# Dense expert dispatch on one core: gates loaded first, x in three loads, and a first store that waits for a load

## The chip, the cores and the metric

The kernel runs on one core of one Trainium2 chip. The metric is device time in microseconds (us) of one execution of the program; lower is better. A profiled execution also gives a span, from the first to the last instruction of the program, which is a little shorter than the device time of the same execution.

## The reference

```python
x: (8, 256, 512) float32;  gate_weights: (8, 256, 8) float32
gate_weights = gate_weights / (np.sum(gate_weights, axis=-1, keepdims=True) + 1e-8)
output = x[:, :, None, :] * gate_weights[:, :, :, None]     # (8, 256, 8, 512) float32
```

Every token has a row of 512 numbers and eight gates. The gates are normalised to a sum of one, and the row is written out eight times, once scaled by each gate. So 4.19 MB of x and 0.07 MB of gates come in, and 33.55 MB go out: the output is eight times as large as the input, and there is one multiplication for each number written.

## The kernel before, in words

**Tiling.** The 2048 tokens are dealt to 128 partitions, 16 consecutive ones to each. From here on "token j" means the j-th of the 16 of every partition, so one token is 128 rows of 512 numbers. All of x (`x_all`) and of the gates (`g_all`) fit into on-chip memory. The output doesn't; it goes through `ring`, which has ten slots of one token with its eight scaled copies (16 KB in each partition).

**Loads (L46 to L48).** ScalarE's queue (ACT) issues the gates. SyncE's queue (SP) issues the first five tokens of x (`HEAD = 5`) and then the other eleven. All of the 16 DMA engines serve both queues; in the profile SP's queue is q1 and ACT's is q10. Every DMA here is split by partition: eight of the 128 partitions fall to each DMA engine, and each partition's contiguous piece is one packet, which is called a row below. A DMA ends on each engine with a packet of 4 bytes, which counts up its semaphore; this is called the closing packet below.

**Gates (L53 to L56).** VectorE (DVE) sums the eight gates of each token, adds 1e-8, takes the reciprocal and multiplies: `gn`. Before that, L50 and L51 have ScalarE load its function table.

**Scaling.** A token is scaled in one of two ways: by eight single operations, one for each expert (`scale_one`: L63 on ScalarE, L65 on VectorE), or by one VectorE operation over all eight experts (`scale_token`, L68). Tokens 0 and 1 are split: experts 0 to 2 on ScalarE and 3 to 7 on VectorE. After that the first token of every chunk goes to ScalarE (L63, eight operations) and all others to VectorE (L68).

**Chunks and stores.** `CHUNKS` lists (first token, number of tokens, first slot). The five chunks hold 2, 3, 3, 4 and 4 tokens, in slots 0-1, 2-4, 5-7, 0-3 and 6-9. After each chunk SP issues one store of it (L87), when both engines are done with it. Chunk 3 writes over slots of chunks 0 and 1, so its operations wait until those stores have landed; chunk 4 writes over two slots of chunk 2 and waits for that store. Slots 8 and 9 are free from the start.

**What sets the order.** On an engine the instructions run in the order of the compiled program. The framework orders them by dependencies and its own estimate, and does not keep strictly to the source: the ten L68 operations run for tokens 3, 4, 6, 7, 14, 9, 15, 10, 11 and 13. SP's queue holds the two loads of x and the five stores in source order; an SP instruction that waits holds up all that come after it on SP.

Of the kernel before, what the change touches and what calls it, by code (L numbers as in the profile page):

```python
# [1 line left out]

# [4 lines left out]

SLOTS = 10
HEAD = 5
CHUNKS = ((0, 2, 0), (2, 3, 2), (5, 3, 5), (8, 4, 0), (12, 4, 6))  # L10


@with_exitstack
def kernel(
    ctx: ExitStack,
    tc: tile.TileContext,
    x: bass.AP,
    gate_weights: bass.AP,
    out: bass.AP,
):  # L20
    nc = tc.nc
    P = 128

    B, S, D = x.shape
    E = gate_weights.shape[-1]
    J = B * S // P

    fp32 = mybir.dt.float32
    mult = mybir.AluOpType.mult

    x_v = x.flatten_outer_dims().rearrange("(p j) d -> p j d", p=P)
    g_v = gate_weights.flatten_outer_dims().rearrange("(p j) e -> p j e", p=P)
    out_v = out.rearrange("b s e d -> (b s) e d").rearrange(
        "(p j) e d -> p j e d", p=P
    )

    pool = ctx.enter_context(tc.tile_pool(name="pool", bufs=1))

    g_all = pool.tile([P, J, E], fp32)
    x_all = pool.tile([P, J, D], fp32)  # L40
    ring = pool.tile([P, SLOTS, E, D], fp32)
    gsum = pool.tile([P, J, 1], fp32)
    gn = pool.tile([P, J, E], fp32)
    warm = pool.tile([P, 1], fp32)

    nc.scalar.dma_start(out=g_all, in_=g_v)  # L46
    nc.sync.dma_start(out=x_all[:, 0:HEAD, :], in_=x_v[:, 0:HEAD, :])
    nc.sync.dma_start(out=x_all[:, HEAD:J, :], in_=x_v[:, HEAD:J, :])  # L48

    nc.vector.memset(warm, 0.0)  # L50
    nc.scalar.copy(out=warm, in_=warm)  # L51

    nc.vector.reduce_sum(out=gsum, in_=g_all, axis=mybir.AxisListType.X)  # L53
    nc.vector.tensor_scalar_add(out=gsum, in0=gsum, scalar1=1e-8)  # L54
    nc.vector.reciprocal(out=gsum, in_=gsum)  # L55
    nc.vector.tensor_tensor(  # L56
        out=gn, in0=g_all, in1=gsum.to_broadcast([P, J, E]), op=mult
    )

    def scale_one(engine, j, e, slot):  # L60
        o_ap, s_ap = ring[:, slot, e, :], gn[:, j, e : e + 1]
        if engine is nc.scalar:
            nc.scalar.mul(out=o_ap, in_=x_all[:, j, :], mul=s_ap)  # L63
        else:
            nc.vector.tensor_scalar_mul(out=o_ap, in0=x_all[:, j, :], scalar1=s_ap)  # L65

    def scale_token(j, slot):
        nc.vector.tensor_tensor(  # L68
            out=ring[:, slot, :, :],
            in0=x_all[:, j : j + 1, :].to_broadcast([P, E, D]),  # L70
            in1=gn[:, j, :].unsqueeze(2).to_broadcast([P, E, D]),
            op=mult,
        )

    for j0, m, s0 in CHUNKS:
        for i in range(m):
            j, slot = j0 + i, s0 + i
            if j < 2:
                for e in range(E):
                    on_act = e < 3  # L80
                    scale_one(nc.scalar if on_act else nc.vector, j, e, slot)
            elif i == 0:
                for e in range(E):
                    scale_one(nc.scalar, j, e, slot)
            else:
                scale_token(j, slot)
        nc.sync.dma_start(  # L87
            out=out_v[:, j0 : j0 + m, :, :], in_=ring[:, s0 : s0 + m, :, :]
        )


# [1 line left out]
_INS = ['x', 'gate_weights']  # L93
_OUTS = [((8, 256, 8, 512), 'float32')]


# [23 lines left out]
```

## Time and profile before

| | us |
|---|---|
| median of 8 runs (lowest to highest) | 93.69 (93.59 to 93.81) |
| the profiled execution, device time | 93.61 |
| the profiled execution, span | 91.8 |
| device time outside the span | 1.8 |
| busy in the span: VectorE, ScalarE | 48.6, 25.1 |
| mean rate of all DMAs over the span | 412 GB/s |
| gates, from issue to landing | 5.9 |
| first load of x (1280 KB), from issue to landing | 5.7 |
| second load of x (2816 KB), from issue to landing | 12.0 |
| stores issued at | 11.90, 20.55, 29.22, 50.90, 57.25 |

Times inside the profile are counted from the first instruction. VectorE is busy for half of the span and ScalarE for a quarter, while DMA packets account for almost all of it. In the tables of windows (stretches of the span), "DMA share" is the time of all packets that start in a window, divided by 16 engines and the width of the window. It can be over 1 where many packets start together and run on beyond the window. Share times width is then the time that these packets take on one engine; the rate in GB/s times the width is the bytes that they carry.

### The profile page before, as it was taken

To read this page: it belongs to the slowest core of one execution; us is meant where nothing else is said; L and a number is where in the kernel's file an instruction comes from. 1 tells how busy PE (TensorE), PEld (TensorE's weight loads), DVE (VectorE), ACT (ScalarE), POOL (GpSimd) and SP (SyncE) were. 2 spreads that over 40 slices of the span, in tenths; PEclk is the share of its full clock that TensorE was granted. 3 is DMA by queue.
4 is the path that set the end of the run, shared out by engine and by line. 5 is a ranking of instruction groups with operands and counts; after the bars stand their busy time and mean duration, and the time that the engine had idled before them with its cause. 6 is when DMAs were issued, how large, how long until landed. Compare 5 with 4: busy or idle time off the path is not lost.

```text
span 91.8 us, 131 instructions
## 1 busy us (share of the span) xinstructions
DVE 48.6 (53%) x25; ACT 25.1 (27%) x40; POOL 0.2 (0%) x4
## 2 busy tenths in 40 slices
DVE  0019999999999999999999396000000000000000
ACT  5106999992992000000000299000000000000000
POOL 0000000000000000000000000000000000000000
DMA  4899889999779977987797999999993799999990
GB/s 71 342 490 422 373 385 457 457 457 571 343 343 535 492 343 343 664 364 343 343 685 343 457 457 457 457 457 457 457 428 143 343 457 457 457 457 457 457 457 0
DMA packets 1152, 37.81 MB, mean 412 GB/s; under 512 B 128, under 2 KB 256, under 8 KB 256
## 3 DMA queue, kind: packets, MB, share of 16 engines
q1 hardware_dynamic: 1008, 37.75, 96.1%
q10 hardware_dynamic: 144, 0.07, 0.2%
HBM read 4.26 MB, written 33.55 MB: 412 GB/s over the span
## 4 chain that ended last, share of the span: by engine, by line
DMA 31%; DVE 23%; ACT 5%; issue 2%; ACTq 1%; SPq 0%
DMA out_dram<-ring 25%; DVE ring L68 17%; DMA g_all<-in_gate_weights_dram 6%; ACT ring L63 5%; DVE ring L65 4%; ACTq L115 1%; DVE gn L56 0%; DVE gsum L53 0%; DVE gsum L55 0%; DVE gsum L54 0%; ACTq L63 0%; SPq L87 0%
## 5 line engine op out<-in xcount | busy, mean ns | idle before, releaser
L68 DVE TENSOR_TENSOR ring<-x_all,gn 128x4096 f32<-128x4096 f32 x10 | 43.5, 4421 | 1.4 <-DMA out_dram<-ring 1.4
L63 ACT ACTIVATE ring<-x_all,gn 128x512 f32<-128x512 f32 x38 | 23.6, 709 | 31.0 <-DMA out_dram<-ring 25.9
L65 DVE TENSOR_SCALAR ring<-x_all,gn 128x512 f32<-128x512 f32 x10 | 4.0, 482 | 0.0
L53 DVE TENSOR_REDUCE gsum<-g_all 128x16 f32<-128x128 f32 x1 | 0.3, 286 | 5.8 <-DMA g_all<-in_gate_weights_dram 5.8
L51 ACT ACT_TABLE_LOAD x1 | 1.3, 1283 | 1.1 <-PEq L104 1.1
L50 DVE MEMSET warm<- 128x1 f32 x1 | 0.1, 59 | 0.8 <-PEq L104 0.8
L56 DVE TENSOR_TENSOR gn<-g_all,gsum 128x128 f32<-128x128 f32 x1 | 0.3, 292 | 0.0
L55 DVE RECIPROCAL gsum<-gsum 128x16 f32<-128x16 f32 x1 | 0.3, 253 | 0.0
L51 ACT COPY warm<-warm 128x1 f32<-128x1 f32 x1 | 0.2, 191 | 0.0
L54 DVE TENSOR_SCALAR gsum<-gsum 128x16 f32<-128x16 f32 x1 | 0.2, 175 | 0.0
L104 POOL MEMSET const-bfloat16-1.0<- 128x1 bf16 x1 | 0.1, 102 | 0.0
L104 POOL MEMSET const-uint8-127<- 128x1 uint8 x1 | 0.1, 101 | 0.0
L104 POOL MEMSET const-float32-0.0<- 128x1 f32 x1 | 0.1, 99 | 0.2 <-issue 0.2
L104 POOL MEMSET const-float32-1.0<- 128x1 f32 x1 | 0.1, 98 | 0.0
## 6 DMA issues: line engine op xcount, KB each, us to landing
out_dram<-ring SPq DMA_DIRECT2D x2, 6144.0 KB, 20.0
out_dram<-ring SPq DMA_DIRECT2D x1, 4096.0 KB, 11.2
x_all<-in_x_dram SPq DMA_DIRECT2D x1, 2816.0 KB, 12.0
x_all<-in_x_dram SPq DMA_DIRECT2D x1, 1280.0 KB, 5.7
g_all<-in_gate_weights_dram ACTq DMA_DIRECT2D x1, 64.0 KB, 5.9
out_dram<-ring SPq DMA_DIRECT2D x2, 27.3
```

What stands on the lines that cost most here:

```text
L50: nc.vector.memset(warm, 0.0)
L51: nc.scalar.copy(out=warm, in_=warm)
L53: nc.vector.reduce_sum(out=gsum, in_=g_all, axis=mybir.AxisListType.X)
L54: nc.vector.tensor_scalar_add(out=gsum, in0=gsum, scalar1=1e-8)
L55: nc.vector.reciprocal(out=gsum, in_=gsum)
L56: nc.vector.tensor_tensor(out=gn, in0=g_all, in1=gsum.to_broadcast([P, J, E]), op=mult)
L63: nc.scalar.mul(out=o_ap, in_=x_all[:, j, :], mul=s_ap)
L65: nc.vector.tensor_scalar_mul(out=o_ap, in0=x_all[:, j, :], scalar1=s_ap)
L68: nc.vector.tensor_tensor(out=ring[:, slot, :, :], in0=x_all[:, j : j + 1, :].to_broadcast([P, E, D]), in1=gn[:, j, :].unsqueeze(2).to_bro ...
L104: nc = _bacc.Bacc("TRN2", target_bir_lowering=False, num_devices=1)
L115: with _tile.TileContext(nc) as tc:
```

## The change

The gates move from ACT's queue to SP's, ahead of everything there. The first load of x shrinks from five tokens to two (`HEAD = 2`, 1024 KB) and moves to ACT's queue. The rest of x is split at token 13 (`TAIL`): SP loads tokens 2 to 12 (2816 KB, called the body below) and then tokens 13 to 15 (768 KB, the tail). The store of chunk 0 gets a dependency on the body's load: SP may not issue it until the body has landed. Token 3 was one VectorE operation over all experts; now experts 0 and 1 of it go to ScalarE and 2 to 7 to VectorE, as single operations. Token 2 stays with ScalarE's eight operations. Operations, chunks, slots and stores are otherwise the same.

```diff
-HEAD = 5
+HEAD = 2
+TAIL = 13
...
-    nc.scalar.dma_start(out=g_all, in_=g_v)
-    nc.sync.dma_start(out=x_all[:, 0:HEAD, :], in_=x_v[:, 0:HEAD, :])
-    nc.sync.dma_start(out=x_all[:, HEAD:J, :], in_=x_v[:, HEAD:J, :])
+    nc.sync.dma_start(out=g_all, in_=g_v)
+    nc.scalar.dma_start(out=x_all[:, 0:HEAD, :], in_=x_v[:, 0:HEAD, :])
+    body_load = nc.sync.dma_start(
+        out=x_all[:, HEAD:TAIL, :], in_=x_v[:, HEAD:TAIL, :]
+    )
+    nc.sync.dma_start(out=x_all[:, TAIL:J, :], in_=x_v[:, TAIL:J, :])
...
+            elif j == 2:
+                for e in range(E):
+                    scale_one(nc.scalar, j, e, slot)
+            elif j == 3:
+                for e in range(E):
+                    scale_one(nc.scalar if e < 2 else nc.vector, j, e, slot)
             elif i == 0:
...
-        nc.sync.dma_start(
+        store = nc.sync.dma_start(
             out=out_v[:, j0 : j0 + m, :, :], in_=ring[:, s0 : s0 + m, :, :]
         )
+        if j0 == 0:
+            tc.add_manual_dep(
+                store.ins,
+                body_load.ins.name,
+                mybir.DependencyInfo(
+                    mybir.DependencyClass.Sync, mybir.DependencyReason.DATA
+                ),
+                reason="no store among the loads",
+            )
```

In the compiled order of the changed kernel VectorE runs 16 single operations instead of 10 and then L68 nine times, for tokens 4, 6, 7, 9, 14, 15, 10, 11 and 13. ScalarE runs 40 single operations instead of 38. SP's queue holds gates, body, tail and the five stores.

## The prediction, made before the changed kernel ran

> **What bounds the kernel now.** I begin with the page: the row of DMA slices, and the queues.
>
> ```profile
> DMA  4899889999779977987797999999993799999990
> ...
> q1 hardware_dynamic: 1008, 37.75, 96.1%
> ```
>
> Packets of SP's queue alone fill 96.1% of the 16 engines' span, while VectorE is busy for 53%. The low digits are coarse: a packet counts where it starts, and packets of 64 KB take 2.4 us. Next the chain of work, in order of time:
>
> ```profile
> 0.72 5.87 DMA g_all<-in_gate_weights_dram
> ...
> 7.76 4.05 DVE ring L65 x10
> 11.81 11.34 DVE ring L68 x3
> ...
> 29.22 22.91 DMA out_dram<-ring
> 52.13 0.02 issue
> ```
>
> It names gates, VectorE and a store, but is a chain of dependencies only. The store issued at 29.22 landed at 52.13 because it stood behind two others. What matters is when the DMA engines had nothing to move. The windows show it, first where the loads end and the first store begins, then where chunk 3's store begins:
>
> ```profile
> 12.38:12.48 0.10, 0.10 (x1) 0.10 (x1) 0.00 (x0) 1.00 0.05 0
> 12.48:12.58 0.10, 0.10 (x1) 0.10 (x1) 0.00 (x0) 1.00 0.02 0
> 12.58:12.68 0.10, 0.10 (x1) 0.10 (x2) 0.00 (x0) 1.00 0.02 0
> 12.68:12.74 0.06, 0.06 (x1) 0.06 (x2) 0.00 (x0) 1.00 0.01 0
> 12.74:12.90 0.16, 0.16 (x1) 0.16 (x2) 0.00 (x0) 1.00 7.60 3277
> ```
>
> ```profile
> 51.60:51.75 0.15, 0.00 (x0) 0.00 (x0) 0.00 (x0) 1.00 0.05 0
> 51.75:51.90 0.15, 0.00 (x0) 0.00 (x0) 0.00 (x0) 1.00 16.40 6991
> 54.20:54.36 0.16, 0.16 (x1) 0.16 (x1) 0.00 (x0) 1.00 15.15 6554
> ```
>
> The last two columns are DMA share and GB/s. From 12.38 to 12.74 no data packet starts; there are only closing packets of the loads, most of them early (mean 12.51). From 12.74 to 12.90 all 16 engines begin the store (3277 GB/s x 0.16 us = 16 rows of 32 KB), on the mean at 12.80. So **the engines idle 0.29 us on the mean**, and 0.16 us if the last closing is set against the last beginning. The second place is alike: closings about 51.66, beginnings about 51.81, 0.14 us. From 12.74 to 51.74 the share is 1.00, as from 51.75 to 90.48. The kernel is DMA traffic from end to end, and these two gaps and the start are all that an order of work can win.
>
> **Prices from the rows.** A 32 KB row takes 7.60 x 0.16 = 1.216 us on its engine, a 64 KB row 15.15 x 0.16 = 2.424. So data moves at 27.1 bytes per ns, with 0.008 us over for each row. By this a 10 KB row costs 0.386, one of 4 KB (new head) 0.16, of 6 KB (tail) 0.235, of 512 bytes (gates) 0.027; these are estimates. A row of the body has the 22 KB of the old second load. The first rows (window 1.74:2.20, share 2.14, so 0.98 us each) show 0.60 us of start-up. SP's issue to first row is 12.74 - 11.90 = 0.84 us. From the last closing packet to landing is 0.4 us (12.74, against 1.16 + 12.0).
>
> **Gates first, and a smaller head.** Before, gates rows alternate with 10 KB rows of x, so both land together: issue 0.72 + 5.9 for the gates, 0.73 + 5.7 for the head. After, if the two queues alternate again, eight pairs of 0.027 + 0.16 follow the start: 1.94 (mean first row) + 0.60 + 1.50 = 4.0, with spread and landing (0.7: before, gates and head close between 5.68 and 6.10, and the gates land at 6.6) **4.7 instead of 6.6**. The chain from gates to the first scaling is unchanged (7.76 - 6.59 = 1.17), so scaling starts at 5.9 and chunk 0 is ready to issue 4.14 us later, as now (11.90 - 7.76): 10.0. The gain is hidden by itself, because no store can move data before the loads are through. It is cover. Swapping queues costs no issue: SP still has its second DMA at 1.16, the tail's issue (0.43) follows at 1.6, and ACT's 0.39 comes ahead of the same table load.
>
> **Three loads.** Each engine serves 32 load rows instead of 24, and one closing packet more: 8 x 0.008 + 0.01 = **+0.07 us**, on the path. Otherwise the bytes are the same.
>
> Here a rule speaks against the change. The Trainium skill, "DMA: Bandwidth & Descriptors", section "Rules for kernel authors", asks for at least 1 MiB per DMA, and its section "Anatomy of one DMA" fits 2.0 us of fixed time to each DMA of the GpSimd path; the 768 KB tail would by that make the sum 95.4. But here the second load landed 6.7 us after the first (13.16 against 6.43) with 2.88 MB: 430 GB/s, hence no fixed time between queued DMAs.
>
> **The added wait.** Before, the loads' last closings lie from 12.38 to 12.74; after, 0.07 later. The body closes 8 x 0.235 + 0.01 = 1.89 earlier: 10.56 to 10.92. It lands at 11.3; SP issues about 0.07 later (52.13 to 52.21 is such a wake-up) at 11.4, and the first row is ready at 12.24, the last at 12.40. The loads end from 12.45 to 12.81, so **the first gap closes**, with 0.05 us to spare at the tightest. The tail covers the landing, the issue and the first row of the store. Behind the wait on SP stand only the four later stores, which nothing wants before 18. It binds (11.3 against 10.0), but 0.5 us before today's issue.
>
> **Tokens 2 and 3.** They now wait for the body: VectorE idles from 10.0 to 11.4 and ScalarE a little longer. Then VectorE does six single operations, 0.40 each by their spacing (4.05 for ten), then token 4 at 4.34 (39.10 for nine): 18.2. ScalarE does ten at 0.61: 17.5. Chunk 1 can be issued at 18.3 against 20.55, needed by 21.6 (chunk 0 ends near 22.5, less 0.84). Chunk 3 is complete after token 11, the eighth large operation: 11.4 + 2.4 + 8 x 4.34 = 48.5, against 50.90. Its store is needed by 51.66 - 0.84 = 50.8, less what the stream gains: 50.5. So **the second gap closes too**. Without this move chunk 3 would be at 11.4 + 9 x 4.34 = 50.5, on the edge. Waits on slots cost VectorE nothing: token 9 comes at 26.8 (chunk 0 landed by 23), token 10 at 39.8 (chunk 1 by 38).
>
> **The sum.** On the mean engine -0.29 - 0.14 + 0.07 = -0.36; on the slowest, -0.16 - 0.14 + 0.07 = -0.23. The last engine ends the kernel, but engines change places, so I take the middle, -0.30. The profiled execution (93.61, span 91.8 and 1.8 around it) becomes 93.31; it lay 0.08 under the median, so I forecast **93.4**. No row shows how the start-up changes with small rows: it may save some of its 0.60 or cost as much again. I take no change, since the first rows wait for a first read either way.
>
> **Rivals.**
> *The head comes late* (slower). Gates and body are in one queue. If the head's rows come a little later, the gates' rows are through first, and the head's rows alternate with 22 KB rows of the body, 0.835 us each. With n such rows the head lands at about 4.7 + 0.85n, and the store is issued 4.2 us after. Up to n = 3 (7.3, issue 11.5) it is hidden. At n = 5 the store is issued at 13.2, its first row is 14.0 instead of 12.8: +1.2 - 0.14, 94.7. At n = 8 the issue is at 15.7: +3.7 - 0.14, 97.2. For it: the gates' eight rows last only 0.22 us, and the body is issued just 0.43 after them. Against it: ACT's gates stood one for one among SP's rows from the first (both DMAs landed within 0.2 us), and the two issues ran side by side (0.38 and 0.39 us, a lone store 0.35).
>
> On this point the Trainium skill, "Perfetto Trace Analysis", section "DMA Instruction — HWDGE (DVE, Sync)", says that the generator of descriptors is shared and locked by one DMA at a time. That would put the head a generation behind the gates and favour this rival, 94.7; the two issues of equal length speak against a long lock.
>
> *Small rows are paid by latency* (slower). If up to eight first pairs each pay a fresh read instead of streaming, part of 8 x (0.60 - 0.19) = 3.3 us is added; at a quarter, 94.2. The 512-byte rows now between rows of x speak against it.
>
> *The wait bites* (no gain). If landing or wake-up takes 0.4 us more than now, the store misses the tail's cover, and the first gap stays: 93.6 to 93.8.
>
> *The change does nothing.* If the slowest engine alone decides and loses at the start what it gains, or if the store queued behind the tail anyway: 93.6. The wait itself may be empty, as SP's queue serves its rows in order.
>
> *A cheaper start.* If small first rows save 0.3 of the 0.60: 93.1.
>
> **How the numbers follow.** Forecast (93.2 to 93.6) 0.50; cheaper start 0.10; head late 0.17; latency 0.08; wait bites or nothing 0.15. A measurement of this kernel can tell about 0.2%, 0.19 us, from no change, so faster means under 93.50. From the forecast 0.42 falls there, with the cheaper start 0.52. Same (93.50 to 93.88): 0.08 from the forecast, 0.13 from the fourth and fifth, 0.02 from mild late heads, 0.23. Slower is the rest, 0.25. The range, 93.0 to 94.7, takes in the cheap start, the late head up to five rows and a third of the full latency.
>
> **What would show it.** Right: gates landed near 4.7, the first store issued near 11.4 on the body's landing, data rows right behind the loads' closings, chunk 3 issued before 50, no gap near 51.6. Wrong: a head that lands after 7.4, a first store released by VectorE or ScalarE, first rows much over 1 us in sum, or load rows slower than 27 bytes per ns.

## The result, and the profile after

The changed kernel takes 93.23 us (median of 10 runs, 93.14 to 93.31) against 93.67 for the kernel before (28 runs, 93.53 to 93.81). The ratio is 0.9952, with a 95% interval from 0.9944 to 0.9960: 0.48% faster, 0.44 us. Its profiled execution took 93.14 with a span of 91.4; before, it was 93.61 and 91.8.

The page of the changed kernel, DMA slices and queues:

```profile
DMA  1999899999789879987997999999999985999990
...
q1 hardware_dynamic: 1152, 37.29, 94.7%
q10 hardware_dynamic: 144, 0.52, 1.7%
```

These rows look like those of before, since a half-microsecond gap doesn't show in slices of 2.3 us. The chain of work, in order of time, does show a change:

```profile
0.72 0.37 SPq L47
...
1.15 10.08 DMA x_all<-in_x_dram
...
11.26 2.47 DVE ring L69 x6
13.72 13.01 DVE ring L72 x3
...
26.80 25.08 DMA out_dram<-ring
```

It no longer runs through gates and single scaling operations, but through the load of the body (landed at 11.23) to token 3. The timeline gives the moments that the prediction named:

```profile
4.07 0.29 DVE L57 TENSOR_REDUCE gsum<-g_all 128x16 f32<-128x128 f32 x1 [3.22 <-DMA g_all<-in_gate_weights_dram]
...
5.21 4.05 DVE L69 TENSOR_SCALAR ring<-x_all,gn 128x512 f32<-128x512 f32 x10
11.25 11.14 ACT L67 ACTIVATE ring<-x_all,gn 128x512 f32<-128x512 f32 x18 [2.25 <-DMA x_all<-in_x_dram]
11.26 2.47 DVE L69 TENSOR_SCALAR ring<-x_all,gn 128x512 f32<-128x512 f32 x6 [1.99 <-DMA x_all<-in_x_dram]
11.32 46.01 SPq L97 DMA_DIRECT2D out_dram<-ring  x5
13.64 34.77 DVE L72 TENSOR_TENSOR ring<-x_all,gn 128x4096 f32<-128x4096 f32 x8
```

Gates land at 4.05 instead of 6.6, scaling starts at 5.21, chunk 0 is done before 9.3, then both engines idle until the body lands at 11.23. SP issues the first store at 11.32. Its own waits confirm who released it:

```profile
SPq L97 <- DMA x_all<-in_x_dram: 9.2, 1, 9.2
```

Last, the windows around the two former gaps:

```profile
11.74:12.18 0.44, 0.44 (x3) 0.44 (x2) 0.00 (x0) 1.00 1.03 433
12.18:12.50 0.32, 0.32 (x2) 0.32 (x2) 0.00 (x0) 1.00 1.94 826
12.50:12.84 0.34, 0.34 (x2) 0.34 (x2) 0.00 (x0) 1.00 2.37 1018
51.02:51.53 0.51, 0.00 (x0) 0.00 (x0) 0.00 (x0) 1.00 4.76 2056
```

No window is without data any more (last column). By the trace's packets, the loads close from 12.19 to 12.83 (mean 12.50) and the store's rows begin from 12.19 to 12.84 (mean 12.51): 0.006 behind on the mean. Chunk 3's rows likewise begin 0.006 behind chunk 2's closings (51.02 to 51.51). Both gaps are gone.

That isn't the whole gain. From the latest first store row to the last closing packet of the kernel it took 77.78 us before and takes 77.31 now, 0.46 less, of which the second gap explains some 0.15. The rest lies in the store rows: 1.224, 1.822 and 2.426 us on the mean for 32, 48 and 64 KB before, 1.214, 1.817 and 2.420 after. There are 8, 16 and 16 of them on each engine: 0.08 + 0.08 + 0.10 = 0.26 us. On the engine that comes last, whose rows now cost 1.213, 1.815 and 2.418, it is about 0.3. The prediction had no such term, and it became the first thing to explain.

### The profile page after: what moved, and what is told of

Read it like the earlier page. It is cut to its first block, busy times and chain, and to the rows that moved or that the text cites. A ratio compares the mean times of both kernels' runs of the same rounds, so it can differ in the third digit from the quotient of the medians.

```text
span 91.4 us, 140 instructions
## 1 busy us (share of the span) xinstructions
DVE 46.7 (51%) x30; ACT 26.4 (29%) x42; POOL 0.2 (0%) x4
## 4 chain that ended last, share of the span: by engine, by line
DMA 38%; DVE 17%; ACT 5%; ACTq 1%; SPq 0%; issue 0%
DMA out_dram<-ring 27%; DVE ring L72 14%; DMA x_all<-in_x_dram 11%; ACT ring L67 5%; DVE ring L69 3%; ACTq L134 1%; SPq L47 0%; ACTq L67 0%; SPq L97 0%
## 5 line engine op out<-in xcount | busy, mean ns | idle before, releaser
L72 DVE TENSOR_TENSOR ring<-x_all,gn 128x4096 f32<-128x4096 f32 x9 | 39.2, 4420 | 3.6 <-DMA out_dram<-ring 3.6
L67 ACT ACTIVATE ring<-x_all,gn 128x512 f32<-128x512 f32 x40 | 25.0, 708 | 29.4 <-DMA out_dram<-ring 24.6
L69 DVE TENSOR_SCALAR ring<-x_all,gn 128x512 f32<-128x512 f32 x16 | 6.5, 481 | 2.0 <-DMA x_all<-in_x_dram 2.0
```

The lines of the kernel that those rows point to most:

```text
L72: nc.vector.tensor_tensor(out=ring[:, slot, :, :], in0=x_all[:, j : j + 1, :].to_broadcast([P, E, D]), in1=gn[:, j, :].unsqueeze(2).to_bro ...
```

## The experiments

Two theories of mine stood at the start. One is the prediction's: the kernel is one stream of rows, served in the order of SP's queue. From this follows that the added wait has no value of its own. The other answers the cheaper rows: in the kernel before, the first gap makes all 16 engines begin the store within 0.14 us of each other, in the changed kernel they begin over 0.64 us, and rows cost more when the engines run in step. It holds only in part, as will be seen. Its rival was that the cheaper rows come from something else in the change. "Before" below is the kernel before beside the same runs.

### The changed kernel without its wait

```diff
-        if j0 == 0:
-            tc.add_manual_dep(store.ins, body_load.ins.name, ...)
```

> The changed kernel without the dependency of the first store on the body's load. Theory (the kernel is one stream of DMA rows, and SP's queue serves its rows in order): the store is issued near 9.4, its rows stand behind the tail's, no gap between loads and store, and the time is that of the changed kernel, 93.1 to 93.3. Rival (the wait protects the loads from the store): load rows get slower or the loads land later than in the changed kernel, and the time is 93.5 or more.

Measured: 94.14 (7 runs, 93.75 to 94.39) against 93.73, ratio 1.0043 (1.0028 to 1.0059). The store was issued at 9.53. The windows of this kernel, the last two columns DMA share and GB/s:

```profile
9.00:10.40 1.40, 0.44 (x2) 0.18 (x1) 0.00 (x0) 1.00 0.94 407
...
11.40:11.90 0.50, 0.48 (x2) 0.48 (x1) 0.00 (x0) 1.00 0.98 184
11.90:12.40 0.50, 0.50 (x3) 0.50 (x2) 0.00 (x0) 1.00 0.73 184
12.40:12.88 0.48, 0.48 (x2) 0.48 (x2) 0.00 (x0) 1.00 0.82 346
```

Until 10.4 the loads run at 407 GB/s, from 11.4 to 12.4 at 184. No store row has begun then; the first does at 12.90. So the store is indeed served after the loads, and the loads are slowed all the same, by a store that has moved no data yet. They close on the mean at 13.31 instead of 12.50. By the packets the slowing is a stretch of its own: between 10.64 and 12.39 the 6 KB rows cost up to 0.83 us, and the 50 that start later cost 0.234 again, though the store's rows still wait behind them. So it begins soon after the store's rows can have reached the engines (9.53 + 0.84 = 10.37, with the 0.84 that a store into idle engines took before) and is over some 2 us later. My theory of the wait falls, and the rival holds: **the wait is worth 0.9 us**, more than the whole change.

### The kernel before with token 3 alone changed

```diff
+            elif j == 3:
+                for e in range(E):
+                    scale_one(nc.scalar if e < 2 else nc.vector, j, e, slot)
```

> The kernel before with one part alone: token 3 as single operations, experts 0 and 1 on ScalarE. The first gap stays (store issued near 11.9), the second goes, as chunk 3 is issued near 49.5. Theory (store rows are dearer where all 16 engines begin together, as after the first gap): only 0.13 to 0.17 is won, 93.50 to 93.55, and the rows stay near 1.218 us for 32 KB and 2.424 for 64 KB. Rival (the cheaper rows of the changed kernel, 1.214 and 2.420, come from the shorter work on VectorE or from the absent second gap): 93.25 to 93.35 with the cheaper rows.

Measured: 93.54 (9 runs, 93.41 to 93.67) against 93.73, ratio 0.9978 (0.9969 to 0.9988), 0.19 us. The windows around the two places:

```profile
12.24:12.81 0.57, 0.57 (x3) 0.57 (x2) 0.00 (x0) 1.00 0.02 0
12.81:12.96 0.15, 0.15 (x1) 0.15 (x2) 0.00 (x0) 1.00 8.12 3495
...
51.68:51.85 0.17, 0.00 (x0) 0.00 (x0) 0.00 (x0) 1.00 14.31 6168
```

The first gap is there (no data from 12.24 to 12.81, then all 16 rows within 0.15), the second isn't: by the packets chunk 3 begins 0.006 behind chunk 2. Rows stay dear, 1.223, 1.822 and 2.423. So neither VectorE's shorter work nor the closed second gap cheapens rows; what remains is the way the first store begins.

### The changed kernel without a tail

```diff
-TAIL = 13
+TAIL = 16
...
-    nc.sync.dma_start(out=x_all[:, TAIL:J, :], in_=x_v[:, TAIL:J, :])
```

The first store now waits for all of x.

> The changed kernel with body and tail as one load, so that the first store waits for all of x. Theory: without the tail's cover the engines idle for landing, issue and first row: loads close near 12.4 on the mean, land near 13.1, the store is issued at 13.2 and its rows begin at 14.05 to 14.2, a gap of 1.6 on the mean engine and 1.4 on the slowest; and since all engines then begin together, store rows cost 1.218 and 2.424 again, some 0.25 in all: 94.6 to 94.9. Rival (row prices have nothing to do with the common beginning): 1.214 and 2.420 rows, 94.4 to 94.6. If the wait is hidden anyway: 93.2.

Measured: 94.77 (4 runs, 94.73 to 94.82) against 93.73, ratio 1.0112 (1.0097 to 1.0127).

```profile
12.24:12.74 0.50, 0.00 (x0) 0.00 (x0) 0.00 (x0) 1.00 0.02 0
12.74:14.04 1.30, 0.91 (x3) 0.91 (x2) 0.00 (x0) 1.00 0.00 0
14.04:14.20 0.16, 0.16 (x1) 0.16 (x1) 0.00 (x0) 1.00 7.62 3277
```

A gap of 1.67 us on the mean engine (closing 12.44, beginning 14.11), then rows in step, at 1.224, 1.822 and 2.423. Theory on both counts, and the price of the tail's cover: about 1.5 us against the changed kernel.

### One load for the rest of x, and no wait

Both edits above together.

> The changed kernel with body and tail as one load and without the dependency. Theory: eight rows and one closing packet fewer on each engine, 0.07 us; the store, issued near 9.4, stands behind the load in the same queue; no gap: 93.1 to 93.2. Rival (a store among the loads costs): 93.5 or more.

Measured: 94.07 (5 runs, 93.96 to 94.13), ratio 1.0035 (1.0023 to 1.0047). The rival again: the store is issued at 9.92, and the loads close from 12.21 to 13.67 instead of from 12.19 to 12.83.

### Queues of gates and head swapped back

```diff
-    nc.sync.dma_start(out=g_all, in_=g_v)
-    nc.scalar.dma_start(out=x_all[:, 0:HEAD, :], in_=x_v[:, 0:HEAD, :])
+    nc.scalar.dma_start(out=g_all, in_=g_v)
+    nc.sync.dma_start(out=x_all[:, 0:HEAD, :], in_=x_v[:, 0:HEAD, :])
```

> The changed kernel with the queues of gates and head as before: gates on ACT, head on SP ahead of body and tail. Theory (gates land early because the rows they alternate with are 4 KB instead of 10 KB, not because they come first): gates land near 4.5, chunk 0 is ready before 10, and the wait on the body decides as in the changed kernel: 93.1 to 93.35. Rival (gates must be first in SP's queue): gates land near 6, scaling starts near 7.2, the store is issued after 11.5 and a gap stays: 93.5 or more.

Measured: 93.24 (5 runs, 93.07 to 93.34) against 93.65, ratio 0.9954 (0.9940 to 0.9968): the changed kernel's time. Which queue takes the gates has no part in the gain, though it moves the gates: they land at 4.73 here, 0.7 later than in the changed kernel, and with five tokens in the head they landed at 6.6. That the gain needs the smaller head is an inference, as no run has the new loads with the old head: with gates at 6.6 chunk 0 was ready at 11.9, and a first store at 11.87 (the tail of two below) gave 93.51. This profile also refines the theory of rows in step. Its 64 KB rows cost nearly as much as those of before, 2.423 on the mean, with the engines spread over 0.3 to 0.36 us. But sorted by their place, the first 15 engines pay 2.421 to 2.424, and the last, which trails by 0.1 us, pays 2.418. From the latest first store row to the end this kernel takes 77.31, like the changed one. So it is not the mean that counts but whether the last engine is in the pack.

### Loads and wait alone

The changed kernel with the branch for `j == 3` taken out again, so that token 3 is one VectorE operation.

> The changed kernel with token 3 as one VectorE operation again, so that loads and wait stand alone. VectorE then has nine large operations from 11.26 on; chunk 3 is issued near 50.4, its first row is ready at 51.2, while chunk 2's rows end from 51.0 to 51.5. Theory: on the slowest engine nothing is lost, but early engines wait up to 0.2 and the engines draw together, so the last rows cost a little more: 93.25 to 93.35. Rival (the second gap stays as it was): 93.35 to 93.45. Second rival (token 3 has no part): 93.2.

Measured: 93.28 (5 runs, 93.21 to 93.29) against 93.65, ratio 0.9961 (0.9948 to 0.9975). So loads and wait bring nearly all. The profile of this run also decides on the rows within one kernel. Its windows, beside the same row of the changed kernel:

```profile
13.40:14.05 0.65, 0.65 (x1) 0.65 (x2) 0.00 (x0) 1.00 1.87 807
51.27:51.52 0.25, 0.00 (x0) 0.00 (x0) 0.00 (x0) 1.00 9.78 4194
```

The second 32 KB rows cost 1.87 x 0.65 = 1.215, as in the changed kernel; their engines began over 0.65 us. Chunk 3 was issued at 50.44, a little late for the early engines, and all 16 began within 0.24 us. From there the rows are dear: 9.78 x 0.25 = 2.445 for the first, 2.425 on the mean of all 16, against 2.420 in the changed kernel.

### Other tails

```diff
-TAIL = 13
+TAIL = 14
```

and likewise 12, 11 and 10.

> The changed kernel with a tail of two tokens (TAIL = 14). The body lands 0.6 later, the first store is issued near 11.9 and its first rows begin from 12.76 to 12.9; loads end from 12.2 to 12.8. Theory (a short gap on the early engines makes all begin together, and rows then cost 1.218 and 2.424 again): 93.4 to 93.6. Rival (the slowest engine alone counts, row prices are not tied to the common beginning): 93.25 to 93.3.

> The changed kernel with a tail of four tokens (TAIL = 12). The body lands 0.6 earlier, the first store is issued near 10.7 and its rows reach the engines near 11.55, while load rows go on until 12.5. Theory (load rows are slowed from the moment a store's rows stand behind them; without any wait these 2.4 us of overlap cost 0.9): 1.0 us of overlap costs 0.25 to 0.4, 93.45 to 93.65. Rival (a little overlap costs nothing, as the tail of three already overlaps): 93.15 to 93.3.

To tell causes of the slow loads apart, two longer tails followed, with the changed kernel beside them.

> The changed kernel with a tail of six tokens (TAIL = 10). The body lands near 9.4, so the wait hardly binds and the first store is issued near 9.55, as in the kernel without a wait, but with the body already landed. It tells two causes of the slow load rows there apart. Cause A (a store issued while over 2 us of load rows are still ahead of it slows them): as without a wait, 93.9 to 94.3, load rows of the tail well over their price. Cause B (the store must not be issued while an earlier load than the one ahead of it is unfinished, that is, with more DMAs outstanding): 93.0 to 93.25 and tail rows at their price.

> The changed kernel with a tail of five tokens (TAIL = 11). The body lands near 10.0, the first store is issued near 10.15, between the kernel without a wait (9.53) and the tail of four (10.87). Cause A (rows of the load still ahead): between their times, 93.3 to 93.9. Cause B (body unfinished): 93.0 to 93.25.

> The changed kernel itself, on the chip and beside the same runs of the kernel before as the tails of five and six tokens: 93.15 to 93.35, a ratio near 0.995. It is the measure for the two others.

| tail, tokens | first store issued | loads close, mean and last | us | ratio (95% interval) |
|---|---|---|---|---|
| 2 | 11.87 | 12.34, 12.62 | 93.51 | 0.9989 (0.9979 to 1.0000) |
| 3 (changed kernel) | 11.32 | 12.50, 12.83 | 93.23 | 0.9952 (0.9944 to 0.9960) |
| 3, again | 11.44 | 12.60, 12.89 | 93.20 | 0.9947 (0.9934 to 0.9961) |
| 4 | 10.87 | 12.53, 12.84 | 93.06 | 0.9938 (0.9925 to 0.9952) |
| 5 | 10.16 | 12.58, 12.76 | 93.21 | 0.9961 (0.9943 to 0.9979) |
| 6 | 9.71 | 12.97, 13.37 | 93.68 | 0.9999 (0.9987 to 1.0011) |
| 3, no wait | 9.53 | 13.31, 13.74 | 94.14 | 1.0043 (1.0028 to 1.0059) |
| none, no wait (from above) | 9.92 | 12.78, 13.67 | 94.07 | 1.0035 (1.0023 to 1.0047) |

The tail of two came out as the theory of rows in step has it: a short gap, beginnings within 0.15 us, rows at 1.224, 1.823 and 2.423. With the tail of four I was wrong: a microsecond of overlap costs nothing. The times of the two longer tails fit neither cause well: 93.68 lies below what cause A gave for the tail of six, and 93.21 for the tail of five lies where cause B put it. The profile of the tail of six decides: its body had landed (9.62) when the store was issued, and the loads were slowed nevertheless:

```profile
9.00:10.40 1.40, 1.23 (x4) 0.96 (x3) 0.00 (x0) 1.00 0.99 421
...
11.90:12.40 0.50, 0.50 (x2) 0.50 (x2) 0.00 (x0) 1.00 0.48 172
```

So cause B falls. Cause A fits with a limit below its 2 us. With the issue at 10.87 or later, and in the profile also at 10.16, the loads close on time; from 9.9 on down they are slowed, and the more the earlier. (The tail of five had runs from 93.07 to 93.58, as if on the edge.) Counted from where the store's rows should reach the engines, 0.85 after issue as with idle engines, up to 1.6 us of load still ahead was free (tail of five), and 1.7 (one load, no wait) or 1.9 (tail of six) was not.

### The head held back

```diff
-    nc.scalar.copy(out=warm, in_=warm)
+    copied = nc.scalar.copy(out=warm, in_=warm)
+    head_load = nc.scalar.dma_start(out=x_all[:, 0:HEAD, :], in_=x_v[:, 0:HEAD, :])
+    tc.add_manual_dep(head_load.ins, copied.ins.name, ...)
```

> The changed kernel with the head's load held back on ACT until after the function table and the small copy (issue near 2.6 instead of 0.7), so that its rows meet the body's. Theory (the two queues alternate row by row): eight head rows stand between 22 KB rows, about 1.0 us each from 3.5 on; the head lands near 12, the first store is issued near 16.2, its first row begins near 17 instead of 12.8: 97.4 to 97.8. Rival (a load in a queue of its own gets through by bytes, not by rows): it lands near 6 and nothing changes, 93.2.

Measured: 98.61 in one run, against 93.78. The head was issued at 2.24; the timeline shows when it landed:

```profile
2.24 0.36 ACTq L55 DMA_DIRECT2D x_all<-in_x_dram  x1
...
12.85 6.85 ACT L75 ACTIVATE ring<-x_all,gn 128x512 f32<-128x512 f32 x11 [10.64 <-DMA x_all<-in_x_dram]
12.86 6.42 DVE L77 TENSOR_SCALAR ring<-x_all,gn 128x512 f32<-128x512 f32 x16 [9.07 <-DMA x_all<-in_x_dram]
17.00 0.35 SPq L105 DMA_DIRECT2D out_dram<-ring  x1
```

ScalarE and VectorE waited for x until 12.8, and the store went out at 17.0. The direction is the theory's and the loss larger than its 97.8. By the packets, each engine served three to five body rows, mostly four, before the first row of the head, which began between 6.24 and 7.09, and only then alternated one for one. The formula had no such delay; its likely reason, rows that an engine has already taken on, is not shown. On alternation itself the Trainium skill ("DMA: Bandwidth & Descriptors", section "Queues, rings and completion order") says that an engine goes round its queues packet by packet, with typically 9 to 17 descriptors to a packet. Here, once the head's rows had begun, the turn came after every single row.

## Why the prediction was right, point by point

- **What bounds the kernel, and the two gaps**: right. Each part that closed a gap brought time (0.19 for the second alone), and each that opened one cost time (1.5 without the tail's cover).
- **Gates first, smaller head**: right that this is cover. (The new head is 512 KB, not the 1024 KB named with the change; the prediction's 4 KB rows have it right.) Gates landed at 4.05, not 4.7, and scaling started at 5.21, not 5.9; the gates' rows ran ahead of the head's instead of alternating evenly (by the packets they close from 3.16 to 3.74, the head's from 3.63 to 4.21). With the queues swapped back they landed at 4.73 and scaling started at 5.89, the very numbers of the forecast, and the time was the same.
- **Three loads, +0.07**: can't be told. The loads closed on the mean at 12.50, not 12.58, but at 12.60 in the changed kernel's other profile, so single executions differ by more than the term.
- **The added wait**: right in time (landing 11.23 for 11.3, issue 11.32 for 11.4, first rows from 12.19 for 12.24) and in effect on the gap.
- **Tokens 2 and 3**: right. Chunk 3 was issued at 48.48 (48.5 forecast). Beside the new loads this part brings little: 93.28 without it, 93.2 with it.
- **The sum**: -0.30 forecast, -0.44 measured. The step that was mis-sized is "Otherwise the bytes are the same": I left the price of the store rows as it was. From the latest first store row to the last closing packet, which is the slowest engine's part, the runs give

| kernel | engines begin the first store over | us from there to the end |
|---|---|---|
| before (with second gap) | 0.14 | 77.78 |
| before with token 3 | 0.14 | 77.63 |
| no tail; tail of two | 0.15 | 77.62; 77.62 |
| head held back | 0.15 | 77.63 |
| one load, no wait | 1.45, then 0.32 for chunk 3 | 77.47 |
| loads and wait alone | 0.65, then 0.24 for chunk 3 | 77.39 |
| changed; again | 0.64; 0.60 | 77.31; 77.32 |
| tails of four, five, six | 0.70, 0.44, 0.64 | 77.31 |
| queues swapped back | 0.50 | 77.31 |
| no wait | 0.85 | 77.31 |

  On this engine the second gap is worth 0.15 and the common beginning after the first gap 0.31, while the latest first row itself moved only from 12.89 to 12.84 (not at all in the changed kernel's other profile, 12.89). So my -0.16 + 0.07 for the first gap, on the slowest engine, should have been -0.05, and -0.31 was missing: -0.05 - 0.15 - 0.31 = -0.51 at the last closing packet, where it went from 90.67 to 90.15. The largest term is thus one that I had put at nothing, while the first gap itself brought less than I counted: that -0.30 came near -0.44 is in part luck.
- **"The wait itself may be empty, as SP's queue serves its rows in order"**, part of a rival: wrong. The order is kept, yet without the wait the loads are slower and the kernel is 0.9 us slower than with it. I had taken order of service for absence of influence.
- **The head comes late**: right that it didn't happen, wrong in the price: 98.6 where the formula gave 97.2 at its worst, though with a head issued 1.5 us later than the rival had it.

No version is clearly better than the changed kernel. The tail of four (93.06) beats the kernel before by 0.62% (0.48 to 0.75), but its interval overlaps that of the changed kernel, and the two were measured on different chips.

## What to carry to other kernels

When the DMA engines are busy from end to end, look for the half microseconds in which they have no data, at the joints between loads and stores, and work out landing, issue and first row against the rows still queued. Don't issue a large store while much of a load is still ahead of it, even in the same queue; let it wait for a part of the load whose remainder just covers the store's way, which here was 1.9 to 3.1 us of rows (tails of three to five tokens). Then compare packet times before and after, because a price that one takes for constant may depend on how the engines were started.

## What the hardware showed unexpectedly

Store rows had two prices. Where all 16 engines began the first store together, within 0.16 us and after a gap, the means were 1.223 to 1.224 us for 32 KB and 2.423 to 2.426 for 64 KB. Where the first store followed the loads without a gap, over 0.44 us or more, 32 KB rows cost 1.213 to 1.214, and the engine that came last paid 2.418 for 64 KB, but for the two kernels named below. Part of it is single rows; in the kernel before, the second row after the first gap and the first after the second:

```profile
13.90:14.12 0.22, 0.22 (x1) 0.22 (x2) 0.00 (x0) 1.00 5.67 2383
51.75:51.90 0.15, 0.00 (x0) 0.00 (x0) 0.00 (x0) 1.00 16.40 6991
```

5.67 x 0.22 = 1.247 and 16.40 x 0.15 = 2.460, where the changed kernel has

```profile
13.40:14.05 0.65, 0.65 (x2) 0.65 (x2) 0.00 (x0) 1.00 1.87 807
```

1.87 x 0.65 = 1.215 and (row 51.02 further up) 4.76 x 0.51 = 2.428 with the rounding of so wide a window, 2.419 by the packets. Two kernels whose rows became dear in mid-run tie the price to the beginning and not to the rest of the kernel: loads and wait alone, after chunk 3 began within 0.24 us, and the one without wait and tail, whose 64 KB rows cost 2.424 to 2.428 on every engine after a late chunk 3, against 1.214 and 1.815 for 32 and 48 KB ahead of it.

What exactly makes them dear stays open. Running in step fits the swapped queues, where no queue ran empty and yet the pack paid and only the engine behind it didn't. A restart after an empty queue fits the kernel without wait and tail better: its engines were still 0.32 us apart then, and all paid. Nor does any run here show by what means a store that has moved no data yet slows a load to 184 GB/s, or why the slowing ends after some 2 us.
